# Forget and decay sums moved from slab pairs 2 and 3 to slab pair 5, and the output gate built from 8 blocks instead of 32 pieces

## The chip, the cores and the metric

The kernel is one program on one core of a Trainium2 chip. Five engines work side by side, each through its own queue in a fixed order: PE (TensorE, matrix products into PSUM), DVE (VectorE), ACT (ScalarE), POOL (GpSimd) and SP (SyncE, which issues the DMAs here). An instruction that waits for a semaphore holds up everything behind it on its engine. The metric is the device time of one execution in microseconds (us); the time before is the median of three runs.

## The reference

One decoder layer on 1024 positions of width 1024 in float32, with two token mixers that read the same normalised input `h`:

- `ada = silu(c) @ w_ada + b_ada` is split into shift, scale and gate; `h = rmsnorm(x) * (1 + scale) + shift`.
- `proj = h @ w_in` (8472 columns) is split into `z_ssm`, `xbc`, `dt_raw`, `q`, `k`, `v`, `z_att`, `f_logit` and `g_logit`.
- The SSD branch passes `xbc` through a causal convolution of four taps and silu. `dt = softplus(dt_raw + dt_bias)`, `a = -exp(a_log) * dt`, and the running sums of `a` within chunks of 128 positions (`a_cs`) give the decays `exp(a_cs[l] - a_cs[s])` of the chunk products and of the states carried between chunks.
- The forgetting attention adds `f_cum[q] - f_cum[k]` to its logits, where `f_cum` is the running sum of `log_sigmoid(f_logit + b_f)` over all positions.
- `merged = sigmoid(g_ssm) * (y_ssm @ w_proj_ssm) + sigmoid(g_att) * (y_att @ w_proj_att)`, then `x + gate * (merged @ w_out)` and a final RMSNorm. The kernel multiplies `gate` into the columns of `w_out`.

## The kernel before

**Precision.** A float32 operand is split into a high and a low part (`split`, lines 101 to 104): ACT casts to the high part (line 102), and POOL, or DVE where named, subtracts it from the operand for the low part (line 103). A product then takes three matmuls: high by high, high by low, low by high (lines 499 to 501 in the slab pairs).

**Stages.** Normalisation of `x` and two directly computed slabs (to about 123 us), the slab pairs of the input projection (to about 560 us), the SSD branch with three `v` slabs and seven `q`/`k` slabs placed between its steps (to about 790 us), the attention (to about 1070 us), and the two branch projections and the output.

**Slab pairs.** `PAIRS` lists 19 pairs of slabs of 128 output columns. The loop at line 619 takes them in order, n = 0 to 18: pair 0 is two merge gates, pair 1 the convolution slabs with B and C, pair 2 two merge gates, pair 3 two convolution slabs, pair 4 two `z` slabs, pair 5 two convolution slabs, pair 6 `z`, pair 7 convolution, pair 8 merge gates, pair 9 convolution, pair 10 merge gates, pairs 11 and 12 `z`, pairs 13 to 16 `z_att`, pairs 17 and 18 merge gates. `c_pair` (lines 463 to 522) computes a pair by seven block products instead of eight, in the order f1, f6, f7, f5, f4, f2, f3. Each has 12 matmuls into a PSUM bank of its own. In the trace their operands tell them apart: f1 and f2 read `hh` and `wh`, f3 `hh` and `sh`, f6 `thb` and `sh`, f7 `tha` and `wh`, f5 `tha` and `sh`, f4 `thb` and `wh`. DVE combines them (L508 for f6, L509 for f7, L511 and L512 for f5, L515 for f4, L518 for f2, L521 for f3), ACT copies f1 (L507), and the slab's own closing work follows: for a merge gate a tanh on ACT (L188), for `z` a tanh (L528) and a multiply (L529), for a convolution copies on ACT (L538) and, once the pair is done, ten passes of 1024 columns on DVE (L542, L545, L548) with a tanh between (L547). L481 to L484 on DVE form the weight sums of a pair, L590 to L593 those of later stages (`w_sums`).

**PSUM banks.** Eight banks are handed out in turn, by the count of `bank()`:

```
if len(banks) % 8 in (1, 2, 3):
    return mm_tile()                                             # pool "mm", 3 banks
return pap.tile([P, 512], F32, tag="pp", bufs=5, name="pp")     # pool "pp", 5 banks
```

So f7, f5 and f4 of pair 2 are in `mm` and its other four products in `pp`; of pair 5, f1, f6, f7, f5 and f4 are in `pp`, f2 and f3 in `mm`. The small sums below take a `pp` bank directly.

**SBUF buffers.** Tiles of 1028 columns for almost everything that passes through (`ev`, line 83) share four buffers: `tmp`, `a`, `gb`, `wga`, `gbias`, the merge gates' `gt`, the `z` slabs' `zt`, the convolution's `xp` and `cv`. Raw weights (`wr`) have four buffers, the high and low parts (`wh`, `wl`) five each.

**The forget and decay sums.** At n = 2 `tmp` is loaded from `d_scr`, and `dt_chain` (line 366) computes the softplus of `dt` and of the forget logits in some 25 small DVE operations (L372 to L394) and one on ACT. Its end forms the running sums of the forget logs by PE: `tmp` columns by a triangle (L396) and the chunk offsets by ones (L397), a DVE copy (L399) and a store to `f_scr` (L400), which the attention reads at 785.6 us and later. At n = 3 `ssm_sums` (line 404) forms the sums of `a`: L407 on DVE into an `ev` tile, three products (L412 to L414), then copies and exponentials (L416 to L429) and stores to `a_scr` and `e_scr`, which the SSD stage reads.

**The output gate.** `out_gate` (line 552) multiplies the gate columns of `w_ada` by silu(c) and adds them up over k. A call handles 256 output columns: two loads of 128x1024 (four k-blocks of 256 columns each), and eight DVE operations of 256 columns (L562 for the first, L565 for the rest). Four calls stand at pair 10, 11, 12 and 12. `gate_sum` at pair 13 sums `gb` over the partitions by a product with ones, 512 columns at a time (L574), adds the bias and halves it (L575, L576).

**What sets the order.** The kernel is written in one program order, and a planner, which simulates the engines, writes each engine's queue out before the launch. It gives an instruction its turn by its place in the program (some parts are raised) and by when its operands and buffers come free in the simulation. It waits for nothing at run time, so where an engine is later than simulated, those that stand in a queue behind its consumer are late too.

Of the kernel before, what the change touches and what calls it, by code (L numbers as in the profile page):

```python
# [24 lines left out]
F32 = mybir.dt.float32  # L25
F32R = mybir.dt.float32r
AF = mybir.ActivationFunctionType
ALU = mybir.AluOpType
# [3 lines left out]
P = 128  # L32
S = 1024
D = 1024
# [35 lines left out]
def build(ctx, tc, t):  # L70
    nc = tc.nc
    V, A, G, PE, SP = nc.vector, nc.scalar, nc.gpsimd, nc.tensor, nc.sync

    const = ctx.enter_context(tc.tile_pool(name="const", bufs=1))
# [8 lines left out]
    def ev(name):  # L83
        return evp.tile([P, 1028], F32, tag="ev", bufs=4, name=name)
# [63 lines left out]
    ones = const.tile([P, P], F32, name="ones")  # L148
    V.memset(ones, 1.0)
    tri = const.tile([P, P], F32, name="tri")  # L150
# [4 lines left out]
    cols = const.tile([P, NROWS], F32, name="cols")  # L155
# [4 lines left out]
    f_scr = dram.tile([64, P], F32, name="f_scr")  # L160
# [172 lines left out]
    dec = const.tile([P, NC, SH], F32, name="dec")  # L333
    ed = const.tile([P, NC, 8], F32, name="ed")

    def gate_slab(j):
# [26 lines left out]
    with tc.tile_pool(name="pa", bufs=1, side="right") as pa, \  # L363
            tc.tile_pool(name="pap", bufs=1, space=PSUM) as pap:

        def dt_chain(dtf, tmp):
# [20 lines left out]

            lf = tmp[:, 192:256].rearrange("p (h c) -> p h c", h=8)
            pre = tmp[:, 256:320].rearrange("p (h c) -> p h c", h=8)
            V.tensor_scalar(out=lf, in0=v[:, :, 16:24].rearrange("p c h -> p h c"), scalar1=-1.0, scalar2=None,  # L390
                            op0=ALU.mult)
            V.memset(pre[:, :, 0:1], 0.0)
            for c in range(1, 8):
                V.tensor_tensor(out=pre[:, :, c:c + 1], in0=pre[:, :, c - 1:c], in1=lf[:, :, c - 1:c], op=ALU.add)  # L394
            ps = pap.tile([P, 512], F32, tag="pp", bufs=5, name="pp")
            PE.matmul(ps[0:64, 0:P], lhsT=tmp[:, 192:256], rhs=tri, start=True, stop=False)  # L396
            PE.matmul(ps[0:64, 0:P], lhsT=tmp[:, 256:320], rhs=ones, start=False, stop=True)  # L397
            ft = tmp[0:64, 320:320 + P]
            V.tensor_copy(out=ft, in_=ps[0:64, 0:P])  # L399
            SP.dma_start(out=f_scr, in_=ft)  # L400

            V.tensor_copy(out=dt, in_=v[:, :, 0:16])

# [148 lines left out]
        def out_gate(gb, g):  # L552

            gb = ev("gb") if gb is None else gb
            gc = slice(g * 256, (g + 1) * 256)
            for hf in range(2):
                wa = ev("wga")[:, :1024].rearrange("p (k c) -> p k c", k=4)
                SP.dma_start(out=wa, in_=t["w_gate"][g, hf])
                for kk in range(4):
                    k = hf * 4 + kk  # L560
                    if k == 0:
                        V.tensor_scalar(out=gb[:, gc], in0=wa[:, kk, :], scalar1=cols[:, k:k + 1], scalar2=None,  # L562
                                        op0=ALU.mult)
                    else:
                        V.scalar_tensor_tensor(out=gb[:, gc], in0=wa[:, kk, :], scalar=cols[:, k:k + 1],  # L565
                                               in1=gb[:, gc], op0=ALU.mult, op1=ALU.add)
            return gb
# [43 lines left out]
        tmp = ev("tmp")  # L611
# [7 lines left out]
        for n, (sa, sb) in enumerate(PAIRS):  # L619
            if n == 2:  # L620
                tmp = ev("tmp")
                SP.dma_start(out=tmp[:, 0:192], in_=d_scr)
                dt_chain(tmp[:, 0:192].rearrange("p (c n) -> p c n", n=24), tmp)
            if n == 3:
                ssm_sums()
# [13 lines left out]
    with tc.tile_pool(name="sd", bufs=1, side="right") as sd, \  # L639
# [152 lines left out]
        for tb in range(8):  # L792
            PE.matmul(rps[:, 2 * tb:2 * tb + 1], lhsT=sacc[:, tb * P:(tb + 1) * P], rhs=ones[:, 0:1],
                      start=True, stop=True)
        rc = const.tile([P, 8], F32, name="rc")
        V.tensor_scalar(out=rc, in0=rps[:, 0:16].rearrange("p (a two) -> p a two", two=2)[:, :, 0],
# [400 lines left out]

def _ada_groups(w):

    m = w.shape[1]  # L1200
    return np.ascontiguousarray(w.reshape(2, 4, 128, m, 4, 256).transpose(4, 0, 2, 1, 3, 5)).reshape(4, 2, 128, 4, 256 * m)


def _t_units(w, c):
# [45 lines left out]
```

## Time and profile before

| what | value |
|---|---|
| median of 3 runs | 1305.86 us |
| lowest and highest | 1300.53 and 1307.06 us |
| the profiled execution, its own time | 1302.24 us |
| its span from first to last instruction | 1300.5 us |
| busy: PE / DVE / ACT / POOL | 1182.4 / 934.5 / 594.6 / 759.7 us |
| mean granted TensorE clock | 0.967 |
| DMA traffic | 228.29 MB, 176 GB/s |

Times in the profile count from the start of the span. A row of the order of time gives the start, the duration, the engine, the line, the operation, the tiles (written <- read) and, in square brackets, the idle time of the engine before it with what ended it. A group row gives the busy time and the mean duration of one. PE matmuls overlap, so their durations add up to more than the time that they take.

### The profile page before, as it was taken

Reading aid. Unit: us, or ns where it says so; the run is one execution under the profiler, and the core shown is the slowest. Engines: PE = TensorE matmul, PEld = TensorE weight load, DVE = VectorE, ACT = ScalarE, POOL = GpSimd, SP = SyncE. Lnnn points to the kernel's source line nnn. Section 1 sums busy time; section 2 is a strip of 40 time slices with the busy share of each in tenths; the row PEclk is TensorE's granted clock in tenths of the full one; section 3 lists DMA queues with packets and bytes.
Section 4 is the critical chain, followed back from the end, with each engine's and each line's share of the span. In section 5 each row is a group of like instructions: output and inputs, shape, how many; then the busy total and the mean of one; then the engine's idle time right before and its main releaser. Section 6 shows DMA issues by size and latency. Waiting matters only on the chain. (4 is left out here: it accounts for less than half of the span.)

```text
span 1300.5 us, 18848 instructions
## 1 busy us (share of the span) xinstructions
PE 1182.4 (91%) x6206; PEld 988.6 (76%) x6206; DVE 934.5 (72%) x1610; ACT 594.6 (46%) x1194; POOL 759.7 (58%) x636
## 2 busy tenths in 40 slices
PE   4889929998998899999988999999999998999896
PEld 3678817876876688799878888888887786888685
DVE  6855474976799576546779873555566978999997
ACT  5453313323233233377667743445456453354354
POOL 3226543556666466627878876445446645687666
PEclk9899969999998899999999999999999999999998
DMA  8664541345438375655646648633227518666234
GB/s 343 236 220 137 181 148 63 127 153 175 173 85 301 121 256 186 226 196 157 213 153 186 192 155 294 224 112 99 91 99 232 189 66 304 219 197 196 56 114 145
DMA packets 109022, 228.29 MB, mean 176 GB/s; under 512 B 12362, under 2 KB 20220, under 8 KB 107900
## 3 DMA queue, kind: packets, MB, share of 16 engines
q1 hardware_dynamic: 108924, 227.09, 52.4%
q8 instruction: 49, 0.80, 0.2%
q14 instruction: 49, 0.40, 0.1%
HBM read 159.14 MB, written 67.90 MB: 175 GB/s over the span
## 5 line engine op out<-in xcount | busy, mean ns | idle before, releaser
L103 POOL TENSOR_TENSOR wl<-wr,wh 128x512 fp32r<-128x512 f32 (+1 forms) x188 | 280.2, 1502 | 166.6 <-ACT wh L102 149.8
L102 ACT CAST wh<-wr 128x512 fp32r<-128x512 f32 (+1 forms) x214 | 129.3, 618 | 177.8 <-DMA wr<-w_c 64.7
L103 POOL TENSOR_TENSOR sl<-sr,sh 128x512 fp32r<-128x512 f32 x57 | 91.1, 1605 | 87.4 <-ACT sh L102 74.6
L116 PE MATMUL mm<-hl,wh 128*128 128x512 f32 x288 | 116.8, 405 | 1.8 <-DVE hl L310 1.8
L115 PE MATMUL mm<-hh,wh 128*128 128x512 f32 x288 | 115.8, 407 | 0.4 <-DVE ql L972 0.4
L117 PE MATMUL mm<-hh,wl 128*128 128x512 f32 x288 | 116.1, 404 | 0.0
L140 PE MATMUL mm<-wh,hh 128*128 128x256 f32 (+1 forms) x256 | 74.3, 292 | 4.9 <-DVE tmp L351 4.9
L102 ACT CAST sh<-sr 128x512 fp32r<-128x512 f32 x57 | 33.8, 617 | 93.5 <-DVE sr L482 74.3
L141 PE MATMUL mm<-wl,hh 128*128 128x256 f32 (+1 forms) x256 | 74.5, 292 | 0.0
L142 PE MATMUL mm<-wh,hl 128*128 128x256 f32 (+1 forms) x256 | 74.4, 292 | 0.0
L1027 ACT ACTIVATE pr<-pr,sm 128x1024 f32<-128x1024 f32 (+3 forms) x64 | 49.9, 780 | 51.5 <-DVE sm L1026 42.1
L1030 POOL TENSOR_SCALAR pr<-pr,sm 128x1024 f32<-128x1024 f32 (+3 forms) x64 | 48.8, 765 | 36.0 <-DVE sm L1029 29.3
L1022 DVE CUSTOM_DVE_ANT_0 pr<-lg,fb 128x512 f32<-128x512 f32 (+1 forms) x96 | 51.6, 551 | 21.5 <-PE lg L1021 13.1
L116 PEld LDWEIGHTS mm<-hl,wh 128*128 128x128 f32 x288 | 55.4, 192 | 13.4 <-DVE hl L310 2.6
L117 PEld LDWEIGHTS mm<-hh,wl 128*128 128x128 f32 x288 | 55.3, 192 | 10.9
L1013 POOL TENSOR_SCALAR_AFFINE_SELECT fb<-fb 128x128 f32<-128x128 f32 x64 | 21.0, 330 | 71.9 <-DVE sm L1022 58.0
L1046 DVE TENSOR_TENSOR ptl<-tp,pth 128x512 fp32r<-128x512 f32 (+1 forms) x80 | 50.1, 632 | 17.9 <-ACT pth L1045 17.6
L115 PEld LDWEIGHTS mm<-hh,wh 128*128 128x128 f32 x288 | 54.8, 193 | 10.4 <-DVE ql L972 0.6
L1045 ACT CAST pth<-tp 128x512 fp32r<-128x512 f32 (+1 forms) x80 | 42.4, 543 | 40.5 <-PE tp L1042 31.3
L692 ACT ACTIVATE ab<-ab,acs 128x128 f32<-128x128 f32 x128 | 41.0, 391 | 32.2 <-DMA ab<-a_scr 30.5
L140 PEld LDWEIGHTS mm<-wh,hh 128*128 128x128 f32 x256 | 49.1, 193 | 5.3 <-DVE tmp L351 5.1
L141 PEld LDWEIGHTS mm<-wl,hh 128*128 128x128 f32 x256 | 49.4, 193 | 0.2
(401 smaller groups left out, 3923.5 us busy)
## 6 DMA issues: line engine op xcount, KB each, us to landing
wr<-w_c SPq DMA_DIRECT2D x116, 256.0 KB, 3.5
wa<-w_ada SPq DMA_DIRECT2D x8, 1024.0 KB, 11.3
g_scr<-gt SPq DMA_DIRECT2D x16, 512.0 KB, 4.1
ab<-a_scr SPq DMA_DIRECT2D x32, 256.0 KB, 3.6
gt<-g_scr SPq DMA_DIRECT2D x32, 256.0 KB, 3.2
wr<-w_ps SPq DMA_DIRECT2D x28, 256.0 KB, 2.9
wr<-w_pa SPq DMA_DIRECT2D x28, 256.0 KB, 3.1
wr<-so SPq DMA_DIRECT2D x28, 256.0 KB, 2.7
```

The source lines that it names most:

```text
L102: A.copy(out=hi[:, :n], in_=raw[:, :n])
L103: eng.tensor_tensor(out=lo[:, :n], in0=raw[:, :n], in1=f32(hi[:, :n]), op=ALU.subtract)
L115: PE.matmul(ps, lhsT=hi[:, cs], rhs=xh[k][:, hs], start=(k == 0), stop=False)
L116: PE.matmul(ps, lhsT=hi[:, cs], rhs=xl[k][:, hs], start=False, stop=False)
L117: PE.matmul(ps, lhsT=lo[:, cs], rhs=xh[k][:, hs], start=False, stop=(k == 7))
L140: PE.matmul(o, lhsT=xh[k][:, ts], rhs=hi[:, cs], start=(k == 0), stop=False)
L141: PE.matmul(o, lhsT=xh[k][:, ts], rhs=lo[:, cs], start=False, stop=False)
L142: PE.matmul(o, lhsT=xl[k][:, ts], rhs=hi[:, cs], start=False, stop=(k == 7))
L1022: V.tensor_tensor_reduce(out=pr[:, n0:n1], in0=lg[:, :n1 - n0], in1=fb[:, n0:n1], op0=ALU.add, op1=ALU.min, scale=1.0, scalar=BIG, accum_o ...
L1027: A.activation(out=pr[:, :n], in_=pr[:, :n], func=AF.Exp, scale=-1.0, bias=sm[:, 0:1], accum_out=sm[:, 1:2])
L1030: G.tensor_scalar(out=pr[:, :n], in0=pr[:, :n], scalar1=sm[:, 1:2], scalar2=0.5, op0=ALU.mult, op1=ALU.mult)
L1046: V.tensor_tensor(out=ptl[:, :w], in0=tp[:, :w], in1=f32(pth[:, :w]), op=ALU.subtract)
```

## The change

The end of `dt_chain` becomes a function of its own, `f_sums`, and is called at n = 5 instead of n = 2; `ssm_sums` is called behind it at n = 5 instead of n = 3. The forget logs and their offsets get a constant tile `fl` of 128x128 for this, since `tmp` is given back after `dt_chain`; the later tile `rc` becomes a slice of `fl`. `out_gate` takes two k-blocks of all 1024 columns at a call, so each DVE operation covers 1024 columns and there are 8 of them; the number and size of the loads stay as they are, and the host lays `w_gate` out to match.

```diff
+    fl = const.tile([P, P], F32, name="fl")
...
-            lf = tmp[:, 192:256].rearrange("p (h c) -> p h c", h=8)
-            pre = tmp[:, 256:320].rearrange("p (h c) -> p h c", h=8)
+            lf = fl[:, 0:64].rearrange("p (h c) -> p h c", h=8)
+            pre = fl[:, 64:128].rearrange("p (h c) -> p h c", h=8)
...
+            V.tensor_copy(out=dt, in_=v[:, :, 0:16])
+
+        def f_sums():
             ps = pap.tile([P, 512], F32, tag="pp", bufs=5, name="pp")
-            PE.matmul(ps[0:64, 0:P], lhsT=tmp[:, 192:256], rhs=tri, start=True, stop=False)
-            PE.matmul(ps[0:64, 0:P], lhsT=tmp[:, 256:320], rhs=ones, start=False, stop=True)
-            ft = tmp[0:64, 320:320 + P]
-            V.tensor_copy(out=ft, in_=ps[0:64, 0:P])
-            SP.dma_start(out=f_scr, in_=ft)
-
-            V.tensor_copy(out=dt, in_=v[:, :, 0:16])
+            PE.matmul(ps[0:64, 0:P], lhsT=fl[:, 0:64], rhs=tri, start=True, stop=False)
+            PE.matmul(ps[0:64, 0:P], lhsT=fl[:, 64:128], rhs=ones, start=False, stop=True)
+            V.tensor_copy(out=fl[0:64], in_=ps[0:64, 0:P])
+            SP.dma_start(out=f_scr, in_=fl[0:64])
...
-            gc = slice(g * 256, (g + 1) * 256)
-            for hf in range(2):
-                wa = ev("wga")[:, :1024].rearrange("p (k c) -> p k c", k=4)
-                SP.dma_start(out=wa, in_=t["w_gate"][g, hf])
-                for kk in range(4):
-                    k = hf * 4 + kk
-                    if k == 0:
-                        V.tensor_scalar(out=gb[:, gc], in0=wa[:, kk, :], scalar1=cols[:, k:k + 1], scalar2=None,
-                                        op0=ALU.mult)
-                    else:
-                        V.scalar_tensor_tensor(out=gb[:, gc], in0=wa[:, kk, :], scalar=cols[:, k:k + 1],
-                                               in1=gb[:, gc], op0=ALU.mult, op1=ALU.add)
+            for k in (2 * g, 2 * g + 1):
+                wa = ev("wga")[:, :D]
+                SP.dma_start(out=wa, in_=t["w_gate"][k])
+                if k == 0:
+                    V.tensor_scalar(out=gb[:, :D], in0=wa, scalar1=cols[:, k:k + 1], scalar2=None, op0=ALU.mult)
+                else:
+                    V.scalar_tensor_tensor(out=gb[:, :D], in0=wa, scalar=cols[:, k:k + 1], in1=gb[:, :D],
+                                           op0=ALU.mult, op1=ALU.add)
...
-            if n == 3:
+            if n == 5:
+                f_sums()
                 ssm_sums()
...
-        rc = const.tile([P, 8], F32, name="rc")
+        rc = fl[:, 0:8]
```

More of the change, by code (lines that the diff above doesn't have):

```diff
@@ L1195, in _ada_blocks @@
     return np.ascontiguousarray(w.reshape(8, 128, 2, 8, 128).transpose(3, 1, 0, 2, 4)).reshape(8, 128, 8, 256)
-def _ada_groups(w):
-    m = w.shape[1]
-    return np.ascontiguousarray(w.reshape(2, 4, 128, m, 4, 256).transpose(4, 0, 2, 1, 3, 5)).reshape(4, 2, 128, 4, 256 * m)
 def _t_units(w, c):
@@ L1227 @@
         "w_ada": _ada_blocks(np.stack([i["w_ada"][:, 1024:2048], i["w_ada"][:, 0:1024]], axis=1)),
-        "w_gate": _ada_groups(i["w_ada"][:, 2048:3072].reshape(1024, 1, 1024)),
+        "w_gate": np.ascontiguousarray(i["w_ada"][:, 2048:3072].reshape(8, 128, 1024)),
         "w_c": _c_units(np.concatenate([wz, wxbc, wq, wk, wza, wg], axis=1)),
```

## The prediction

> **What bounds the kernel now.** I read the page's busy shares and slices first, then the list of PE's waits, then the windows around the longest wait.
>
> ```profile
> span 1300.5 us, 18848 instructions
> PE 1182.4 (91%) x6206; PEld 988.6 (76%) x6206; DVE 934.5 (72%) x1610; ACT 594.6 (46%) x1194; POOL 759.7 (58%) x636
> PE   4889929998998899999988999999999998999896
> ```
>
> PE is busy 91% of the span, and one slice of 32.5 us, the sixth, shows 2 tenths. What ended PE's waits:
>
> ```profile
> PE pp L396 <- DVE tmp L390: 26.3, 1, 26.3
> PE mm L499 <- ACT gt L188: 6.5, 1, 6.5
> PE mm L499 <- DVE zt L529: 5.4, 1, 5.4
> ```
>
> The first is the forget sum of pair 2, the other two lie where the output gate is built. PE loses some 118 us in all (span less busy), so 38.2 of them stand in these three rows, and the change touches the cause of each.
>
> ```profile
> 170.80:197.20 26.40, 0.06 (x2) 0.04 (x1) 23.59 (x36) 5.16 (x8) 8.27 (x5) 0.56 0.40 131
> 197.20:201.40 4.20, 4.20 (x11) 3.13 (x12) 1.18 (x8) 0.00 (x0) 0.00 (x0) 0.50 0.00 0
> 220.00:260.00 40.00, 40.00 (x175) 32.49 (x174) 33.53 (x35) 13.35 (x22) 21.34 (x14) 1.00 0.34 109
> 400.00:440.00 40.00, 34.60 (x132) 27.17 (x131) 37.28 (x58) 13.81 (x25) 20.56 (x15) 0.88 0.65 217
> ```
>
> Columns: length, then busy time of PE, PE's weight loads, DVE, ACT and POOL, the granted clock, the DMA share and GB/s. In the first row PE stands and DVE works; after it PE runs 4.2 us at half clock, which loses another 2.1. In 220 to 260 PE is the bound, in 400 to 440 DVE is (93%).
>
> **The forget sum leaves pair 2.** The order of time shows what stood behind L396:
>
> ```profile
> 162.35 0.39 PE L499 MATMUL mm<-tha,wh 128*128 128x512 f32 x1
> ...
> 171.94 1.36 POOL L103 TENSOR_TENSOR wl<-wr,wh 128x512 fp32r<-128x512 f32 x1 [0.31 <-ACT wh L102]
> 177.89 0.68 DVE L481 TENSOR_TENSOR sr<-wr 128x512 f32<-128x512 f32 x1
> 182.63 3.52 POOL L103 TENSOR_TENSOR sl<-sr,sh 128x512 fp32r<-128x512 f32 x1 [9.34 <-ACT sh L102]
> 186.92 0.67 DVE L372 TENSOR_TENSOR tmp<-tmp,hb 128x192 f32<-128x192 f32 x1 [1.89 <-DMA tmp<-d_scr]
> 197.16 1.42 DVE L394 TENSOR_TENSOR tmp<-tmp 128x8 f32<-128x8 f32 x7
> 197.16 0.69 PE L396 MATMUL pp<-tri,tmp 128*64 128x128 f32 x2 [26.34 <-DVE tmp L390]
> ...
> 231.35 0.39 PE L499 MATMUL pp<-hh,wh 128*128 128x512 f32 x1
> 250.77 0.39 PE L499 MATMUL pp<-hh,wh 128*128 128x512 f32 x1
> ```
>
> Pair 2 begins at 162.35 with f7, out of order: its three `mm` products run, and the four in `pp` wait behind L396, whose bank stands ahead of theirs. L396 needs a DVE chain that starts at 186.92, behind pair 1's convolution, and ends at 198.6. None of the four products needs that chain. Pair 4's f1 starts at 231.35 and pair 5's at 250.77, so a pair takes 19.42 us, a product 2.77. From 162.35 to 231.35 are 69.0 us: 14 products make 38.8, the wait 26.3, the half clock 2.1, and 1.8 are left for the sums' own matmuls.
>
> Without the sums PE has 38.8 us of work from 162.35 and could hand over pair 3 at 201.2. What is late next: pair 3's f1 (low part ready at 173.3) follows pair 2's seven products at 181.8 to 184.6, but f6 needs the low part that POOL finishes at 186.15, some 1.5 us later. So the upper bound is an end at 202.7, 28.7 us earlier. The lower bound is set by PSUM: PE has then filled seven banks with pair 2 and the eighth with f1 of pair 3, and they come free through DVE. If DVE does the whole chain first, to 198.6, it combines pair 2's f6 by 199.3; f7 of pair 3 starts there, five products remain, and the pair ends at 213.1, 18.2 us earlier. Which of these, DVE's order decides. The row at 177.89 is a weight sum of pair 3 in the middle of pair 1's convolution, so later work does slip in ahead of the chain when it is ready, and pair 2's products will now be ready from 165 us on. I take 26, nearer the upper end. Of this 1.8 is PE work that only moves to pair 5, so 24.2 count.
>
> DVE can follow: in 220 to 260 it has 6.5 us idle, and it carries the same work as before. The chain itself stays at pair 2; `dt` and `fl` are ready some 50 us ahead of pair 5. Giving `tmp` back after the chain instead of after the store frees an `ev` buffer earlier, which I count as nothing, as pair 3's own tiles don't wait for it in a quoted row.
>
> **The sums arrive at pair 5.** Five matmul groups, seven DVE copies and sums, three exponentials and three stores on SP come along. The forget part has its operands. The decay part begins with L407 on DVE:
>
> ```profile
> 210.27 0.34 DVE L407 SCALAR_TENSOR_TENSOR a<-dt,hb 128x128 f32<-128x128 f32 x1
> ...
> 257.35 0.69 DVE L518 TENSOR_TENSOR mm<-mm,pe 128x512 f32<-128x512 f32 x1
> ...
> 263.04 0.69 DVE L590 TENSOR_TENSOR sr<-wr 128x512 f32<-128x512 f32 x1 [1.84 <-DMA wr<-w_pa]
> ```
>
> ```profile
> 211.26 0.39 PE L499 MATMUL mm<-tha,sh 128*128 128x512 f32 x1
> ...
> 215.38 0.38 PE L412 MATMUL pp<-a,tri 128*128 128x128 f32 x2
> ```
>
> At pair 3 L407 stood behind L518 of the pair ahead (a light one), and PE had run 4.1 us of `mm` products when it came to L412. At pair 5 the pair ahead is pair 4, whose closing work DVE does late, since pair 3's convolution is in the way: its L518 comes at 257.35, so L407 would end at 258.4. On the old clock PE is through with pair 4 at 250.8 and with the forget sum at 251.8. If it comes to L412 at once, it waits 6.6 us; if f2 and half of f3 (pair 5's only `mm` products) go first, as at pair 3, 2.5. Behind L412 stand f1, f6, f7, f5 and f4, all in `pp`. The bounds: nothing, if L407 finds its buffer earlier; and 11.9 if it comes last in DVE's run, which is idle from 261.2 (263.04 less 1.84): 9.4 of waiting and 2.5 of slow clock (below). I take 4.5, between the two orders. The copies behind the products take some 2 us of DVE where the next convolution will need it; between 0 and 2, I take 1. The stores cost nothing, hidden under PE's products: their first reader is past 560 us. On SP they stand ahead of later pairs' weights, which costs only if DVE is late with what they store. Together 5.5.
>
> **The output gate.** The pieces, beside the nearest operations of 1024 columns:
>
> ```profile
> L545 DVE SCALAR_TENSOR_TENSOR cv<-xp,cols,cv 128x1024 f32<-128x1024 f32 x30 | 48.7, 1652 | 0.0
> L565 DVE SCALAR_TENSOR_TENSOR gb<-wga,cols,gb 128x256 f32<-128x256 f32 x28 | 20.8, 741 | 1.1 <-DMA wga<-w_gate 0.6
> ...
> L542 DVE TENSOR_SCALAR cv<-xp,cols 128x1024 f32<-128x1024 f32 x10 | 14.4, 1484 | 5.5 <-ACT xp L538 5.5
> ...
> L562 DVE TENSOR_SCALAR gb<-wga,cols 128x256 f32<-128x256 f32 x4 | 3.2, 810 | 0.7 <-DMA wga<-w_gate 0.7
> ```
>
> Before: 24.0 us of DVE. After, by the means: 7 x 1.652 + 1.484 = 13.0. That frees 11 us of DVE. Where PE feels it:
>
> ```profile
> 396.83 1.27 ACT L188 ACTIVATE gt<-mm,cols 128x512 f32<-128x512 f32 x2 [1.96 <-DVE gb L565]
> ...
> 397.57 0.79 PE L499 MATMUL mm<-thb,wh 128*128 128x512 f32 x1 [6.46 <-ACT gt L188]
> 402.82 0.39 PE L499 MATMUL mm<-hh,wh 128*128 128x512 f32 x1
> 427.81 1.02 PE L574 MATMUL pp<-gb,ones 128*128 128x512 f32 x2
> 434.23 0.80 PE L499 MATMUL mm<-tha,sh 128*128 128x512 f32 x1 [5.40 <-DVE zt L529]
> ...
> 437.29 0.47 DVE L565 SCALAR_TENSOR_TENSOR gb<-wga,cols,gb 128x256 f32<-128x256 f32 x1
> ```
>
> The first wait: PE needs a bank that ACT empties into `gt`, and `gt` takes the buffer of the first `wga`, which four pieces hold; by the means they take 3.0 us, one block 1.5. The wait becomes shorter by 0 to 3; I take 2. The product behind it took 5.25 us (397.57 to 402.82) instead of 2.77, a slow restart of 2.5, and that stays as PE still stands over 4 us.
>
> By the Trainium skill ("TensorE: Matmul & The Clock Gate", Part 1: The HAM clock gate) an idle window of about 3.4 us halves the clock until a busy window has passed. By that rule the trace agrees, with 0.50 after 26.3 us, and a wait cut from 6.5 to under 3.4 would give back 2.5 more, for a sum of 28.2 instead of the 25.7 below.
>
> The second wait, 5.40 with as slow a restart (7.9 together), comes from DVE being behind. Six of the eight blocks lie ahead of it, some 8 us less work, so I expect it gone. Against it stands a new dependence: L574 at 427.81 needed the first two groups only; now each half of `gb` needs all eight blocks. The last piece ended at 437.76. If the last block were no earlier, PE would stand 10.0 us and restart in 2.5, instead of 7.9: 4.6 lost. With 8 us less it ends near 430, about when PE gets there, and pair 13's `mm` products may go ahead. From -4.6 to +7.9 I take +5.
>
> The Trainium skill ("VectorE: DVE Perf Modes", The TRN2 errata) puts a Vector instruction at 58 cycles plus its columns. Counted so, the 24 instructions saved are an estimate of 24 x 58 / 0.96 GHz = 1.5 us, and the second wait would mostly stay: a sum of some 20. The rows speak for more: the means hold waits that a short piece (0.47 at 437.29, 0.74 on average) meets as often as a long one.
>
> **The sum.** 24.2 - 5.5 + 2 + 5 = 25.7 us. The profiled execution took 1302.24, so 1276.5 on its scale; the median of the runs stands 3.6 above it, and the mean of these four executions is 1303.9. I put the median after at 1303.9 - 25.7 = 1278. The rest costs nothing: `rc` in `fl` is written past 780 us, the loads of the gate are as many and as large.
>
> **The rivals.**
>
> - The chain first (20%): pair 2's combining waits for the chain, 18.2 instead of 26. That gives 1286. For it speaks that the chain stands ahead in the program; against it the row at 177.89.
> - The wait moves along (12%): L407 comes last, PE stands 9.4 us at pair 5, with a slow restart: 24.2 - 13.9 + 7 = 17.3, or 1287. It cannot be more, since DVE has nothing else to do from 261.2 and pair 5's own work stands behind L412.
> - It does nothing (6%): the engines behind don't follow, PE fills its banks and stands until pair 3's convolution is where it was. The gate's 7 against 5.5 leave 1302. Against it, DVE's waits there are for PE and DMA.
> - Slower (6%): the SSD stage, where seven `q`/`k` slabs and three `v` slabs cover a dependent chain of 32 steps.
>
> ```profile
> 562.00:786.00 224.00, 210.38 (x1578) 189.56 (x1577) 162.14 (x332) 151.46 (x376) 169.63 (x157) 0.98 0.56 176
> ```
>
> ```profile
> L103 POOL TENSOR_TENSOR m<-ab,m 128x512 fp32r<-128x512 f32 x32 | 45.1, 1414 | 5.8 <-ACT m L102 3.8 <-issue 1.6
> L103 POOL TENSOR_TENSOR wl<-wr,wh 128x512 fp32r<-128x512 f32 x26 | 35.4, 1371 | 10.3 <-ACT wh L102 10.0
> ```
>
> POOL works (169.6 - 35.4) / 32 = 4.2 us a step without the slabs' splits, and the stage takes 7.0. If the planner, with the hand-over 26 us earlier, uses the slabs up a quarter of the stage too soon, eight steps run bare and cost PE up to 4.2 each: 34, or 1312. It decides from seven bare steps. Against it: the slabs are placed by program order, which the change leaves alone.
>
> **How the numbers follow.** 56% for the forecast. Its own range is 1266 (28.7 - 1.8, no new wait, 3 and 7.9 at the gate: 37.8) to 1292 (pair 3 at its lower bound, 18.2 - 1.8, less 5.5, and a gate worth 1: 11.9). To leave out no more than 2 in 10 the range reaches to the other cases, 1264 to 1299. A measurement of this kernel can tell 0.5%, 6.5 us, from no change. Forecast and the first two rivals make it faster, less the tail where both new waits come at once: 0.84; 0.09 for no change; 0.07 slower.
>
> **What would show it.** Right: no wait of PE at L396 over 1 us; pair 2 starts with f1 instead of f7; pair 4's f1 comes at 203 to 206 instead of 231.35; a wait of PE at L412 of 2 to 7 us, ended by L407; the gate's eight operations at 1.3 to 1.7 us each; no wait of PE on L529 beside the gate's sums. Wrong: PE standing over 10 us at the sums in pair 5 or 13; pair 3 ending no earlier than 213; or a loss past 560 us, which none of my terms contains.

## The result and the profile after

The median of four runs is 1287.73 us (1285.95 to 1289.70), against 1303.2 us for four runs of the kernel before (the three shown and one more): a ratio of 0.9881 with a 95% interval of 0.985 to 0.9913, so 1.2% faster, 15.5 us. The profiled execution took 1289.10 us, 13.1 less than that of before.

The head of the page and the list of PE's waits, of the changed kernel (the line numbers have moved: L407 of the decay chain is L408 now, its products L413 to L415, the pairs' matmuls L500 to L502, the `z` multiply L530, the gate's sum L571):

```profile
span 1287.4 us, 18817 instructions
PE 1181.4 (92%) x6206; PEld 989.7 (77%) x6206; DVE 934.6 (73%) x1586; ACT 594.1 (46%) x1194; POOL 761.6 (59%) x636
PE   4789998599889999999988999999999899999896
...
PE mm L500 <- DVE zt L530: 17.6, 1, 17.6
PE mm L500 <- ACT gt L188: 4.3, 1, 4.3
```

PE's work is the same to 1 us. The wait at the forget sum is gone, the longest of the list has a new place, and one of the gate's two waits is left. The hole in the slices is now a 5 in the eighth, not a 2 in the sixth. The order of time shows both places:

```profile
160.91 0.40 PE L500 MATMUL pp<-hh,wh 128*128 128x512 f32 x1
...
201.33 0.39 PE L500 MATMUL pp<-hh,wh 128*128 128x512 f32 x1
...
220.76 0.43 PE L400 MATMUL pp<-tri,fl 128*64 128x128 f32 x2
237.70 0.69 DVE L519 TENSOR_TENSOR mm<-mm,pe 128x512 f32<-128x512 f32 x1
238.30 0.67 DVE L530 SCALAR_TENSOR_TENSOR zt<-zt,mm 128x512 f32<-128x512 f32 x1
239.03 0.80 PE L500 MATMUL mm<-hh,wh 128*128 128x512 f32 x1 [17.62 <-DVE zt L530]
239.50 0.28 DVE L408 SCALAR_TENSOR_TENSOR a<-dt,hb 128x128 f32<-128x128 f32 x1
244.12 0.38 PE L413 MATMUL pp<-a,tri 128*128 128x128 f32 x2
244.71 0.48 PE L500 MATMUL pp<-hh,wh 128*128 128x512 f32 x1
```

Pair 2 starts with its f1, in order, and pair 4's f1 comes at 201.33. PE does the forget sum at 220.76, and its next product, f2 of pair 5, wants a bank that pair 4's f4 holds until the `z` multiply at 238.30. In its queue f1, f6, f7, f5 and f4 of pair 5 come behind L413, and this needs L408, which DVE does at 239.50. The windows, with the columns of the prediction (length; busy PE, weight loads, DVE, ACT, POOL; clock; DMA share; GB/s):

```profile
165.73:241.20 75.47, 56.75 (x241) 45.28 (x240) 74.90 (x93) 25.10 (x42) 41.22 (x25) 0.88 0.41 132
...
239.03:244.60 5.57, 5.57 (x17) 4.46 (x18) 2.14 (x6) 0.65 (x2) 0.51 (x1) 0.56 1.03 357
400.00:440.00 40.00, 40.00 (x171) 31.95 (x170) 28.31 (x38) 12.03 (x21) 22.84 (x16) 1.00 0.54 178
```

DVE works without a gap from 165.73 to 241.20. In the kernel before, the same stretch had DVE idle for a third:

```profile
165.00:241.00 76.00, 49.66 (x210) 39.50 (x209) 50.60 (x79) 21.52 (x37) 30.90 (x22) 0.82 0.32 101
```

That is 25.4 us idle, 76.00 less 50.60. Only 2.8 of them lie in PE's stand (170.80 to 197.20); 20.5 come behind it, from 197.20 to 241, where DVE mostly waited for products that PE, held up, made late. With the change the products come earlier, and the stretch is full.

It is full for a second reason too: a part of the same work takes longer. Some steps of the softplus chain, in the changed kernel, with a POOL operation of that time:

```profile
201.05 3.98 DVE L383 SCALAR_TENSOR_TENSOR tmp<-tmp 128x192 f32<-128x192 f32 x4
203.01 1.40 POOL L103 TENSOR_TENSOR sl<-sr,sh 128x512 fp32r<-128x512 f32 x1
```

And the same steps in the kernel before, where POOL did nothing from 188.7 to 201.4 us:

```profile
193.72 2.33 DVE L382 SCALAR_TENSOR_TENSOR tmp<-tmp 128x192 f32<-128x192 f32 x6
```

Of the chain's nine operations of this kind and size, the five that a POOL operation overlaps take 1.22 us each in the changed kernel and the four others 0.36, as all nine did before. The vector operations of the whole chain take 17.8 us in sum instead of 9.6.

At the gate, 400 to 440, PE now has no idle time:

```profile
L562 DVE SCALAR_TENSOR_TENSOR gb<-wga,cols,gb 128x1024 f32<-128x1024 f32 x7 | 10.8, 1537 | 1.2 <-DMA wga<-w_gate 1.2
L560 DVE TENSOR_SCALAR gb<-wga,cols 128x1024 f32<-128x1024 f32 x1 | 0.8, 754 | 2.5 <-DMA wga<-w_gate 2.5
...
381.57 0.80 PE L500 MATMUL mm<-thb,wh 128*128 128x512 f32 x1 [4.29 <-ACT gt L188]
412.06 1.88 PE L571 MATMUL pp<-gb,ones 128*128 128x512 f32 x4
```

The gate costs DVE 11.6 us instead of 24.0, and both halves of its sum run together at 412.06. What was gained by then is partly lost in the last pairs. First the weight sums that begin a pair, pairs 15 to 18, on DVE in the kernel before (L481) and after (L482), a group over the window 440 to 560 with its first and last start; then PE's waits there, after:

```profile
L481 DVE TENSOR_TENSOR sr<-wr x4: 691/693/693, 464.6 to 536.6; 128x512 f32<-128x512 f32 x4
```

```profile
L482 DVE TENSOR_TENSOR sr<-wr x4: 693/693/694, 445.6 to 518.6; 128x512 f32<-128x512 f32 x4
...
496.42 0.78 PE L500 MATMUL mm<-thb,sh 128*128 128x512 f32 x1 [2.20 <-ACT sh L102]
498.12 0.80 PE L502 MATMUL mm<-thb,sl 128*128 128x512 f32 x1 [0.48 <-POOL sl L103]
521.15 0.50 PE L500 MATMUL mm<-thb,sh 128*128 128x512 f32 x1 [1.44 <-ACT sh L102]
522.85 0.50 PE L502 MATMUL mm<-thb,sl 128*128 128x512 f32 x1 [0.96 <-POOL sl L103]
```

Three steps take 72.0 us before and 73.0 after: 24 us a pair, where PE needs 19.4. In these pairs the output weights' sums (`w_sums` of `o`, sets 0 to 3, ahead of pairs 15 to 18) take turns with the pairs' own weights in the four raw buffers `wr`. The stream of weights is thus slower than PE. It is 19.0 us earlier than before at pair 15 and 18.1 at pair 18, while PE comes 24.4 us earlier to pair 15 and must wait.

Read off the first matmul of a pair, or of the SSD stage, in the order of time (and subtracted before rounding), the gain of the changed kernel is: pair 4, 30.0 us; pair 5, 11.7; pair 6, 8.8; pair 9, 15.8; pair 14, 24.3; pair 18, 18.5; SSD stage, 16.0; span, 13.2. PE was 1.2 us earlier from pair 0 on, ahead of anything that the change touches.

### The profile page after: what moved, and what is told of

Its sections match the earlier page's. It is cut to its first block, busy times and chain, and to the rows that moved or that the text cites. A ratio compares the mean times of both kernels' runs of the same rounds, so it can differ in the third digit from the quotient of the medians.

```text
span 1287.4 us, 18817 instructions
## 1 busy us (share of the span) xinstructions
PE 1181.4 (92%) x6206; PEld 989.7 (77%) x6206; DVE 934.6 (73%) x1586; ACT 594.1 (46%) x1194; POOL 761.6 (59%) x636
## 5 line engine op out<-in xcount | busy, mean ns | idle before, releaser
L103 POOL TENSOR_TENSOR m<-ab,m 128x512 fp32r<-128x512 f32 x32 | 46.6, 1459 | 5.2 <-ACT m L102 3.6
```

The source lines that it names most:

```text
L103: eng.tensor_tensor(out=lo[:, :n], in0=raw[:, :n], in1=f32(hi[:, :n]), op=ALU.subtract)
```

## The experiments

This table shows all kernels, so that the sections can be short: the start of PE's first product of a pair and of the SSD stage (its first product of B and C), the span, the median and its ratio to the kernel before with its 95% interval. Where products of two pairs run mixed (with the sums at 8 around pair 9, with `o` earlier around pair 18), a pair's start is the time by which PE has begun as many matmuls as the pairs ahead of it have. For two of the kernels there is one run only.

| kernel | pair 5 | pair 9 | pair 14 | pair 18 | SSD | span | median | ratio |
|---|---|---|---|---|---|---|---|---|
| before | 250.8 | 336.0 | 457.5 | 535.2 | 564.7 | 1300.5 | 1303.2 | |
| changed | 239.0 | 320.1 | 433.1 | 516.8 | 548.8 | 1287.4 | 1287.73 | 0.9881 [0.985, 0.9913] |
| gate alone | 251.4 | 339.5 | 447.7 | 528.9 | 563.1 | 1297.4 | 1302.57 | 0.9993 [0.9973, 1.0013] |
| sums alone | 239.6 | 320.7 | 443.3 | 520.8 | 553.6 | 1292.4 | 1293.07 | 0.992 [0.9898, 0.9941] |
| decay sums at 3 | 240.8 | 327.1 | 436.9 | 519.7 | 553.8 | 1292.0 | 1293.78 | one run |
| sums at 6 | 223.0 | 333.4 | 437.5 | 520.4 | 554.0 | 1289.9 | 1292.15 | 0.9918 [0.9897, 0.9939] |
| sums at 8 | 222.1 | 332.5 | 439.7 | 517.3 | 551.8 | 1288.3 | 1291.1 | 0.9904 [0.9885, 0.9923] |
| two taps left out | 234.2 | 315.1 | 427.9 | 510.7 | 544.6 | 1284.6 | 1286.3 | one run |
| first tap on ACT | 238.1 | 319.2 | 431.4 | 514.2 | 548.2 | 1287.5 | 1286.27 | 0.9879 [0.9855, 0.9903] |
| `o` later | 240.2 | 322.1 | 434.8 | 512.4 | 549.4 | 1289.6 | 1290.03 | 0.9891 [0.9872, 0.991] |
| `o` later, before | 251.5 | 336.7 | 456.4 | 534.2 | 571.1 | 1310.5 | 1317.44 | 1.0102 [1.0078, 1.0125] |
| `o` earlier | 240.2 | 321.5 | 433.7 | 527.8 | 555.2 | 1293.2 | 1293.85 | 0.9926 [0.99, 0.9952] |
| `o` and gate earlier | 240.5 | 321.1 | 442.7 | 527.8 | 555.3 | 1292.7 | 1294.82 | 0.9951 [0.9931, 0.997] |
| set 3 in the SSD stage | 239.1 | 320.1 | 432.4 | 515.1 | 540.6 | 1303.5 | 1307.72 | 1.003 [1.0014, 1.0047] |

### The two parts apart

The gate alone: the kernel before with the new `out_gate` and its layout of `w_gate`. The sums alone: the changed kernel with the old ones.

```diff
-            gc = slice(g * 256, (g + 1) * 256)
-            for hf in range(2):
...
+            for k in (2 * g, 2 * g + 1):
+                wa = ev("wga")[:, :D]
```

> The kernel before with the output gate by k-blocks alone; the sums stay at pairs 2 and 3. Theory A (each part takes away its own waits of PE, and the weight buffers of pairs 15 to 18 give part of it back): PE still waits 26 us at L396; the gate's 8 operations take 10 to 13 us instead of 24; the wait before f4 of pair 10 is 2 us shorter than 6.5, the one of 5.4 us beside the gate's sums is gone; pair 14 starts 8 to 11 us earlier than 457.5, the end is 4 to 9 us earlier than before. Theory B (after the change the gain at the gate came only because PE arrived there at another time): the gate alone gives under 2 us.

> The changed kernel with the output gate of before (32 pieces). Theory A: pair 4 starts near 201 as after the change, PE waits 17 to 18 us in pair 5, the waits of 6.5 and 5.4 us at the gate are back within 2 us of their size, pair 14 starts 12 to 16 us earlier than 457.5, and the end is 6 to 12 us earlier than before. Theory B (DVE's backlog follows PE through): the waits at the gate grow by what PE gained, and the end is within 4 us of before.

The gate alone brings nothing that can be measured (the interval holds 1), the sums alone 0.8%. PE did gain by the gate: 9.8 us at pair 14 where it was 3.6 behind at pair 9. Up to there Theory A of the first expectation holds (the wait of 6.5 us is 4.3, the one of 5.4 is gone, and a new one of 2.3 stands at the gate's sum); at the end the figure is that of Theory B, since PE lost most of the gain in pairs 17 and 18. The waits there, of the gate alone:

```profile
510.89 0.50 PE L499 MATMUL mm<-thb,sh 128*128 128x512 f32 x1 [1.88 <-ACT sh L102]
...
535.05 0.80 PE L499 MATMUL mm<-thb,sh 128*128 128x512 f32 x1 [3.22 <-ACT sh L102]
```

The SSD stage starts 1.6 us earlier than before. With the sums alone the waits at the gate are still there, at 5.1 and 6.6 us, and the rest comes as its Theory A has it. The gate on top of the sums takes the median from 1293.07 to 1287.73, though the intervals of the two ratios overlap a little. So the gate's gain at pair 14 is real in both settings, some 10 us (443.3 to 433.1; 457.5 to 447.7), and is worth some 5 us at the end in one and nothing that can be measured in the other.

### Where the sums stand

```diff
+            if n == 3:
+                ssm_sums()
             if n == 5:
                 f_sums()
-                ssm_sums()
```

This is the first kernel, with the forget sums at 5 and the decay sums still at 3. The second and third have both at 6 and both at 8 (`n == 6`, `n == 8`).

> The changed kernel with the decay sums left at pair 3, so that only the forget sums move. Theory A (PE's queue waits for whatever small sum stands ahead of the pair's pp products): the wait only moves on, from pair 2 to the decay products at pair 3, where it is 20 to 28 us, since dt itself is ready at 212 only; the end is within 10 us of before, slower than the changed kernel by 5 to 12. Theory B (it is the forget sum's store or bank that costs): no wait above 5 us at pair 3, the end as after the change.

> The changed kernel with both sums one pair later, at pair 6, where no convolution stands between the pair ahead and them. Theory A (the 17.6 us at pair 5 are the sums' place: five of that pair's seven products stand behind them, and the two others wait for banks): PE's longest wait in pairs 4 to 7 falls under 8 us and pair 9 starts 8 to 16 us earlier than after the change; as pairs 15 to 18 cannot follow, the end is 0 to 5 us earlier than after the change. Theory B (DVE works without a gap from 165.7 to 241.2, so PE has to wait that long wherever the sums stand): PE waits 14 us or more in pairs 4 to 6, and pair 9 starts within 4 us of the changed kernel.

> The changed kernel with the forget and decay products at pair 8 instead of 5. Theory A (PE stands in pair 5 because DVE works without a gap from 166 to 241 us and frees the banks late; the sums only show it): without the sums PE runs some products further, up to the 11.7 us of the four that stand behind them, and then waits for banks; pair 9 still starts within 5 us of 320.1, and the time is within 5 us of the changed kernel, 1283 to 1292. Theory B (the place of the sums makes the wait): the waits of pairs 4 to 8 fall from 17.6 to under 6 us, pair 9 starts at 305 to 310, and at pair 14 PE is still 10 us ahead of 433.1.

The wait moves and stays. PE's longest waits from 180 to 340 us, with the decay sums at 3, with both at 6 and with both at 8:

```profile
PE pp L413 <- DVE xp L536: 9.6, 1, 9.6
PE mm L500 <- ACT sh L102: 4.7, 2, 2.4
```

```profile
PE mm L500 <- ACT sh L102: 6.3, 2, 5.1
PE pp L500 <- DVE zt L530: 5.5, 1, 5.5
PE mm L502 <- POOL sl L103: 5.1, 2, 3.6
PE pp L413 <- DVE a L408: 3.3, 1, 3.3
```

```profile
PE mm L500 <- ACT sh L102: 11.2, 2, 9.9
PE pp L500 <- DVE zt L530: 6.8, 2, 5.6
```

With the sums at 6 or 8 pair 5 starts 16 to 17 us earlier than in the changed kernel, as the four products behind L413 are free to run. By pair 9 PE is 12 to 13 us later than there. Nor does the waiting vanish with the sums out of the way: it comes at products whose weights are not split yet (`sh`) and at banks. For pair 6 neither theory holds: the longest single wait is 5.5 us, as Theory A has it, but pair 9 comes 13 us later instead of 8 to 16 earlier. For pair 8, Theory B with pair 9 at 305 to 310 falls, and Theory A is not shown either. It had pair 9 within 5 us, and DVE is idle there for 20.9 of the 113 us from 222 to 335, 11.2 of it until raw weights land, so these waits are not DVE's backlog alone. What makes them in this order is open. Neither place gives a faster kernel than pair 5. With the decay sums at 3 they wait there, but 9.6 us, far less than the old 26.3 and than the 20 to 28 of the expectation. The forget sum's move (with the new gate) gives 9.4 of the 15.5 us by itself, as far as one run, 1293.78 us, can tell.

### Less work for DVE

First, two of the convolution's taps left out in the slabs of pair 3:

```diff
-                for i in range(1, 4):
+                for i in range(1, 2 if j in (0, 1) else 4):
```

> The changed kernel without the last two of the four taps of the convolution in the first two slabs, four vector operations of 1.2 us each: this part of the computation is left out. Theory A (DVE's backlog is the wait): the wait of 17.6 us at pair 5 falls by 4 to 6 us, to 11 to 14. Theory B (the wait hangs on something else than the amount of DVE's work, a transfer or the place of the sums in PE's order): it stays at 16 to 18.

```profile
PE mm L500 <- DVE zt L530: 11.2, 1, 11.2
```

The wait falls by 6.4 us (the expectation had 4 to 6, with 1.2 us for each of the four operations; the taps of the stretch take 7.1 us less in the trace), and the gain stays up to pair 9 (5.0 us) and the SSD stage (4.2). So the amount of DVE's work sets this wait, as far as a profile of one run shows it. Second, work that is only moved:

```diff
-                V.tensor_scalar(out=v, in0=xp[:, 0:S], scalar1=cols[:, R_CW + j:R_CW + j + 1],
-                                scalar2=cols[:, R_CB + j:R_CB + j + 1], op0=ALU.mult, op1=ALU.add)
+                A.activation(out=v, in_=xp[:, 0:S], func=AF.Identity, scale=cols[:, R_CW + j:R_CW + j + 1],
+                             bias=cols[:, R_CB + j:R_CB + j + 1])
```

> The changed kernel with the first tap of each convolution (scale and bias, 1.27 us on DVE) on ACT, which is busy 25 of the 80 us from 165 to 245. Theory A (DVE's backlog sets the wait at pair 5): four such operations leave the stretch without a gap, 5 us, and the wait of 17.6 us falls to 11 to 14; the time falls by 2 to 5 us, less where the stream of raw weights takes it back (then by 0 to 2). Theory B (another cause): the wait stays at 16 to 18 and the time at 1286 to 1290.

```profile
PE mm L500 <- DVE zt L530: 16.0, 1, 16.0
```

The wait falls by 1.6 us, not by the 4 to 7 expected, and the median, 1286.27, cannot be told from 1287.73. By their figures these are the results of Theory B (another cause). The trace shows where DVE's saving went. Up to the `z` multiply DVE is busy 4.5 us less (67.5 instead of 72.0), but it waits 1.9 us for the tap that ACT now makes, so the stretch is 2.6 us shorter. It also begins 1.7 us later (167.40 instead of 165.73), and PE comes 0.6 us later: 2.6 less 1.7 plus 0.6 gives about the 1.6 measured. So the wait still ends with DVE's work, and this run does not speak against that cause.

### The output weights in the last pairs

The kernel with `o` later takes sets 0 to 2 ahead of pairs 16 to 18, and set 3 behind the last pair; it was made from both kernels.

```diff
- 15: [('o', 0)], 16: [('o', 1)], 17: [('o', 2)], 18: [('o', 3)]}
+ 16: [('o', 0)], 17: [('o', 1)], 18: [('o', 2)]}
...
             fb()
+        w_sums("o", 3, gb)
```

> The changed kernel with the output weights' sums one pair later: sets 0 to 2 ahead of pairs 16 to 18 and set 3 behind the last pair, instead of ahead of pairs 15 to 18. Theory A (in the last pairs the weights of the pairs and the output weights share four raw buffers, one set of four each 11.5 us, so that the stream of weights takes 23 to 24 us a pair where PE takes 19.4, and what PE has gained ahead is given back at pairs 17 and 18): the first weight sum of pair 18 comes at 503 to 508 us instead of 518.5, pair 18 starts at 510 to 513 instead of 516.8, the value slab at 532 to 535 instead of 540.7, and the time falls by 4 to 8 us to 1279 to 1284. Theory B (the loss is in the products' own clock or in the transfers that all of this stage makes, whatever their order): the value slab starts within 2 us of 540.7 and the time stays at 1286 to 1290.

> The kernel before with the same later output weights. Theory A: there PE comes to pair 18 late enough for its weights (its waits there are about 1.3 us), so the time falls by 0 to 3 us. Theory B' (the later sums are worth something by themselves, whatever PE's position): the time falls by 4 to 8 us, as much as in the changed kernel.

In the changed kernel the first half came as Theory A has it, if less (the weight sum of pair 18 at 511.5, not by 508): pair 18 starts at 512.4, and its last matmuls run at 532.0 instead of 540.0 (before: 556.0), with the whole lead of 24 us. The time did not follow, 1290.03 us. The order of time, with SP's issues (`SPq`), shows what came next:

```profile
L482 DVE TENSOR_TENSOR sr<-wr x3: 691/694/694, 461.2 to 511.5; 128x512 f32<-128x512 f32 x3
...
526.92 0.33 SPq L89 DMA_DIRECT2D wr<-w_v  x1
529.14 0.42 SPq L89 DMA_DIRECT2D wr<-w_v  x1
530.52 4.88 SPq L89 DMA_DIRECT2D wr<-w_v  x4
537.15 1.20 SPq L89 DMA_DIRECT2D wr<-w_v  x2
538.40 0.95 SPq L646 DMA_DIRECT2D bc<-x_scr  x2
539.87 2.28 SPq L689 DMA_DIRECT2D ab<-a_scr  x2
549.36 0.47 PE L668 MATMUL sp<-ch,m 128*128 128x128 f32 x1 [4.99 <-DMA ab<-a_scr]
```

```profile
537.67 1.33 SPq L645 DMA_DIRECT2D bc<-x_scr  x2
```

The lower row is of the changed kernel. The loads that open the SSD stage (B and C, L645 or L646) stand on SP behind the value slab's raw weights, and these take their turn behind set 3. In both kernels they go out at 538, whenever PE is there. So in the kernel with `o` later the stream through the four raw buffers, not PE, sets the start of the SSD stage. In the kernel before, where both theories expected a gain, the same edit costs 1.0%: its SSD stage starts 6.4 us later (571.1), and the rest of the 14 us is not explained.

Then earlier instead of later, the sets ahead of pairs 14 to 17, once with the gate as it is and once with its pieces at pairs 9 to 11 and its sum at 12:

```diff
- 15: [('o', 0)], 16: [('o', 1)], 17: [('o', 2)], 18: [('o', 3)]}
+ 14: [('o', 0)], 15: [('o', 1)], 16: [('o', 2)], 17: [('o', 3)]}
```

> The changed kernel with the output weights' sums one pair earlier: sets 0 to 3 ahead of pairs 14 to 17, the gate as it is. Theory A' (behind pair 14 the stream of raw weights, 11.5 us a set of four, is the bound, down to the loads for the value slabs and the state stage behind it on SP's queue; it cannot begin before the gate's row is there, at 422 us): with one set fewer between pair 14 and pair 18 the value slab starts 4 to 9 us before 540.7, the state stage 3 to 8 us before 548.8, and the time falls by 3 to 8 us, to 1280 to 1285. Theory B'' (the state stage is held by something that the order of the sets does not touch): the state stage starts within 2 us of 548.8 and the time stays at 1286 to 1290.

> As the one before, and the gate's row one pair earlier too (its pieces at pairs 9 to 11, its sum at pair 12). Theory A': the stream of sets can begin some 15 to 20 us earlier, since the four buffers stood from 410 to 434 us with sets that waited for the gate; the value slab starts 6 to 10 us before 540.7, which is all that PE has to gain there, and the time falls by 5 to 10 us, to 1278 to 1283. Against it stands that DVE gets the eight long gate operations (about 1.6 us each) while pairs 9 to 11 need it: new waits of 3 to 8 us there would take the gain away. Theory B'': 1286 to 1290.

Both medians lie above the changed kernel's, by 6.1 and 7.1 us (for `o` earlier the intervals of the ratios just overlap), and the theory in this form falls: an earlier start does not help the stream. The first weight sum of pair 14, in the changed kernel and with `o` earlier:

```profile
410.41 1.78 DVE L482 TENSOR_TENSOR sr<-wr 128x512 f32<-128x512 f32 x1
```

```profile
434.31 0.69 DVE L482 TENSOR_TENSOR sr<-wr 128x512 f32<-128x512 f32 x1 [3.68 <-issue]
```

Set 0 now stands ahead of pair 14's weights and delays them by 24 us. PE starts pair 14 at 433.7. The lead of 23 us with which the stream entered the last pairs is used up at once. With the gate earlier PE also loses 7 us to it in pair 11 (pair 12 at 400.6 instead of 393.2 with `o` earlier alone), the price that the expectation named. With `o` earlier the weight sums of pairs 14 to 18 start at 434.31, 457.79, 481.03, 505.41 and 516.11: a pair with a set takes 23 to 24 us, the one without 10.7. A set thus costs about the 11.5 us that I had counted, but pair 17's weights come 12 us later than in the changed kernel (493.23), and PE stands for them.

Last, set 3 out of the pairs and into the SSD stage:

```diff
- 17: [('o', 2)], 18: [('o', 3)]}
+ 17: [('o', 2)]}
...
+            if late:
+                e1, e2 = ev("so1"), ev("so2")
+                s1, s2, s4 = e1[:, 0:512], e1[:, 512:1024], e2[:, 0:512]
...
+        w_sums("o", 3, gb, True)
         cb = [sd.tile([P, NC, P], F32, name=f"cb{g}") for g in range(2)]
```

> The changed kernel with the output weights' set 3 out of the pairs: sets 0 to 2 stay ahead of pairs 15 to 17, and set 3 is taken up in the state stage, behind the loads of its first two slabs (its three sums stand in two buffers of the general pool there). Theory A' (the last part is bound by the number of sets that pass the four raw buffers between pair 14 and the value slabs, and a set costs some 11.5 us): the first weight sum of pair 18 comes at 503 to 508 us instead of 518.5, the last pair ends and the state stage's first product starts 6 to 12 us before 548.8, and the time falls by 4 to 10 us, to 1278 to 1284, if set 3 does not take it back inside the state stage. Theory B'' (the state stage's start is held by something that the sets do not touch): it starts within 2 us of 548.8 and the time stays at 1286 to 1291.

The starts came as expected, the time did not. The last pair ends at 533.7 instead of 540.0, and the stage starts at 540.6, with the value slab behind its first products now. But the stage, to the sums of squares behind it, takes 246 us instead of 222. The windows over it, here and in the changed kernel:

```profile
541.00:787.00 246.00, 220.35 (x1606) 199.34 (x1606) 167.53 (x330) 152.93 (x378) 176.33 (x161) 0.96 0.53 170
```

```profile
549.00:771.00 222.00, 205.36 (x1535) 184.39 (x1534) 159.47 (x328) 147.13 (x371) 167.90 (x155) 0.98 0.54 174
```

PE is idle 25.7 us instead of 16.6 and busy 15.0 us longer; it has 71 matmuls more there (the slab that otherwise stands ahead of it), at a clock of 0.96 instead of 0.98. In none of the other thirteen kernels does this stage take more than 224 us. What in the new order costs so much is open.

## Why the prediction was right or wrong

**The time.** 1278 was forecast and 1287.73 measured: inside the range of 1264 to 1299, faster as said, with 15.5 of the 25.7 us. Up to pair 14 the trace shows 23.1 us (24.3 less the 1.2 of the start), 2.6 less than the sum. That this is so near is in part luck: the wait at pair 5 cost far more than its term, and 7.0 us came back in pairs 6 to 8, which no term contained. The rest was lost behind pair 14, in a place that the sum did not contain.

**The forget sum leaves pair 2: right, and a little larger.** No wait at the forget sum, pair 2 in order, pair 4's f1 at 201.33 (203 to 206 said). From pair 2 to pair 4 are 40.4 us instead of 69.0, so 28.6, the upper bound of 28.7 where I took 26. DVE combined pairs 2 and 3 between the steps of the chain, as the weight sum at 177.89 had suggested. The first rival, the chain first, is out.

**The sums arrive at pair 5: the step that failed.** 4.5 us were forecast, and 9.4 of waiting named as the most that it can be. It was 17.6, and 2.3 more for a product at a clock of 0.56 (5.1 us from 239.03 to L413 at 244.12, instead of 2.77). The step that failed is "DVE can follow: in 220 to 260 it has 6.5 us idle", and with it the bound, which took L518 of pair 4 at its old place relative to PE. PE came to the sums 30.0 us earlier, but DVE's closing of pair 4 moved only from 257.35 to 237.70, 19.7 us. The old difference of 6.6 us grew by 10.3 to 16.9, near the 17.6 measured. The account for those 19.7 us comes out. From the weight sum of `w_ps` (at 167.10 before, at 165.73 after) to L518, DVE is idle 22.8 us less (0.5 instead of 23.3), but it is busy 4.5 us longer (71.4 instead of 67.0), though the decay sums' operations have left the stretch; with the start 1.4 us earlier that makes 19.7. So a second part of the sentence failed as well: "it carries the same work as before" holds for the instructions and not for their time, since the chain takes 8.2 us more, beside POOL's operations. Without these the wait would be near the 9.4 that the bound allowed; that is an estimate, 17.6 less 8.2, and no run tests it.

The run with two taps left out bears out that DVE's work sets the wait. PE did not stand at L413 at all: it had already stood one product ahead of it, at f2, whose bank DVE freed late. Of the signs for "right", the wait of 2 to 7 us ended by L407 thus did not come, and my own mark for "wrong", over 10 us at the sums in pair 5, was met.

It cost less than its length. Pairs 6 to 8 took 65.8 us before (270.2 to 336.0) and 58.7 after (261.4 to 320.1). These 7.0 us stood in no term. They fit a backlog that PE now waits out at pair 5 and had to wait out later before, but no run shows that it is the same one. At pair 9 the sums' net is 15.8 less 1.2, so 14.6, against 18.7 forecast. The rival in which the wait moves along had the right kind of wait and, with 1287, the time; its price was 13.9 and the wait's 19.9, so that its sum is right by luck, by what it left out. Its reason why the wait could be no longer (DVE has nothing else to do from 261.2) rests on the same old place of DVE.

**The gate: right up to pair 14.** The first wait fell by 2.2 (2 said) and kept its slow restart; the second went, with no wait on L530 there and both sums at 412.06. DVE's saving was 12.4 us, 11 said. From pair 9 to pair 14 the gain grows by 8.5 us, 7 said. The Trainium skill ("VectorE: DVE Perf Modes", The TRN2 errata) has 58 cycles plus the columns, by which a block would cost an estimated 3.4 pieces. The page adds that this row gives too little and that about 150 cycles were measured in place of the 58, which makes it an estimated 2.9. The trace disagrees as to the means: a block takes 1.45 us and a piece 0.75, 1.9 times as much, and the second wait went. Where no POOL operation overlaps them, a piece takes 0.47 us and an operation of 1024 columns 1.27, 2.7 times; the 14 of 32 pieces that one overlaps take 1.11.

**What no term contained.** Behind pair 14 PE loses 8.4 of its 24.3 us up to the SSD stage and 2.8 more within the rest of the span. For the first part there is a cause that the runs show: the stream of raw weights. PE's lead at pair 14 counts as far as that stream is earlier too, and it was 18 to 19 us earlier. The gate alone, of whose 9.8 us 1.6 are left at the SSD stage, and the kernel with `o` later, where PE keeps its lead to the last pair and the SSD stage starts no earlier, are two sides of that. The traces agree on it: in the eight kernels whose sets stand where they stood, the weight sum of pair 18 is 4.2 to 23.2 us earlier than before, and the SSD stage is earlier by 2.0 to 3.2 us less than that in each. That the stream as a whole is faster in the kernel before (from set 0's first sum to the SSD stage 109.4 us, 114.7 after) is measured and not explained. The 2.8 us are not explained either, and they are no more than the kernels differ by: from the SSD stage's start to the end of the span it takes 735.8 us before and 738.6 after, and 734.3 to 740.2 in the kernels that leave this stage alone. So the sign "a loss past 560 us" was not clearly met. The rival "slower" did not come, though such a loss is possible: with set 3 in the stage, and so another order there, it took 24 us more.

**No better version.** None of the runs can be told from the changed kernel on the good side. With the first tap on ACT the median is 1.5 us lower, well inside the intervals.

## What to carry to other kernels

When a stall of one engine goes, add up the idle time that the engine behind it had during the stall and up to the next place where the first one needs it: that, and not its idle time elsewhere, is how far it can follow. Ask also whether its operations will last as long as before when a third engine works beside them, which the stall had kept quiet. Then go along the whole stage and look for a second stream that the change doesn't move, such as weights through a few shared buffers; what the first engine gains beyond it is waited out there. A wait that appears at a new place should be priced by the positions behind it, since part of it may only be a wait that was due later.

## What the runs showed of the hardware

Short waits cost more than their length. After a wait of 2.20 us and one of 0.48 at 496 to 498 us PE's matmuls went at 0.55 to 0.80 us instead of 0.39 for 6.9 us, with a granted clock of 0.51 (496.42 to 503.36):

```profile
493.83 0.39 PE L502 MATMUL mm<-hh,wl 128*128 128x512 f32 x1
496.42 0.78 PE L500 MATMUL mm<-thb,sh 128*128 128x512 f32 x1 [2.20 <-ACT sh L102]
502.55 0.63 PE L500 MATMUL pp<-tha,wh 128*128 128x512 f32 x1
503.36 0.39 PE L502 MATMUL pp<-tha,wl 128*128 128x512 f32 x1
```

That is some 3 us for 2.7 us of waiting, and after 1.44 and 0.96 us at 521 to 523 they went at 0.63 from 523.96 to 526.95, at a clock of 0.50. The Trainium skill ("TensorE: Matmul & The Clock Gate", Part 1: The HAM clock gate) ties the slow clock to an idle window of about 3.4 us. Here less than that, in two pieces with matmuls between, was enough, so a wait is not free of it by being short.

DVE is slower beside POOL. In the changed kernel's trace, sorted by whether a POOL operation overlaps them, DVE's additions and subtractions (TENSOR_TENSOR, 128x512 float32) whose operands all lie in SBUF take 1.22 us with one (120) and 0.68 without (96). Those with an operand in PSUM take 0.68 us either way (160 and 59). So an order in which POOL works beside DVE can cost DVE time though neither has more to do; for the chain here this is read from the overlap, and no run took POOL's work away to test it.
